# Group-0 chunks of the state-space mixer computed during a reordered convolution, three-block tails split by tokens, and weights loaded ahead of the norms, in a two-layer hybrid block

## The chip, the cores and the metric

The kernel runs on one core of one Trainium2 chip. The metric is the device time of one execution in microseconds. TensorE (PE; its weight loads are PEld), VectorE (DVE), ScalarE (ACT), GpSimd (POOL) and SyncE (SP, which here only issues DMAs) work side by side, each through its own instruction queue in order.

## The reference, cut to what matters

Two layers over 512 latent tokens (`x`) and 256 context tokens (`ctx`) of width 1024. In the last layer only the latent tokens are carried on.

```python
h  = rms_norm(x, w) * (1 + sc_m) + sh_m            # adaLN; the same for the context
ua, ub, ug = split(h @ w_in)                       # neighbourhood attention | SSD | GQA
ya = neighbourhood_attention(ua)
# SSD: z, xbc, dt = split(ub); xbc = silu(depthwise_conv5(xbc)); xs, B, C = split(xbc)
#   per chunk of 128 tokens, both directions, 8 heads in 2 groups:
#   y_diag = ((C B^T) * decay) @ (xs * dt);  y_off = C @ h_enter;  y += d_skip * xs
#   then y * silu(z), RMSNorm
yg = gqa_attention(ug)
x = x + g_m * (concat(ya, yb, yg) @ w_out)
x = x + g_f * swiglu(rms_norm(x) * (1 + sc_f) + sh_f)
```

## The kernel before

Everything is float32. A matrix product is made from three: each operand is split into a rounded high part and the rest, and high*high, high*low and low*high are summed (`proj_ws`, L349; weights stationary, 512 + 256 token columns moving in the first layer, 512 in the last; `proj_as`, L364, has the activations stationary). `load_w` (L341) fetches a weight block by a DMA of SP into a raw buffer (tag `wr`, two of them), ACT writes the high part (L345), DVE the low part (L346), into `wh`/`wl` (three pairs) or `vh`/`vl` (two pairs). A raw buffer is free again when DVE has made the low part. Program order is the order in which raw buffers are asked for. The framework orders the instructions of each engine by a list schedule in program order and by its own clock; `tc.issue_after(i)` puts the instructions of a block behind `i` on `i`'s engine.

A layer runs so. `make_h` (L323) makes the normalised input of 8 blocks of 128 channels. The input projection follows: queries and keys of the neighbourhood attention, `p_kv` (L709), `p_q` (L718), then the eight blocks of the convolution, `p_xbc(b)` (L758), in the order 0 to 7: blocks 0 to 3 are xs (0 and 1 are head group 0), 4 and 5 are B of group 0 and 1, 6 and 7 are C. Between them stand the gate blocks `p_z` (L808), transposes `p_xtr`, `decays` (L821, after block 4), the heads' rotary work, and in the first layer the modulation products `mod_steps` (L213), moved on by `step_md`.

Then comes a loop over attention units (48 in the first layer, 32 in the last): scores into PSUM, maximum (DVE), exponential (ACT), normalisation (POOL, L437), transposes (PE, L447), values (PE, L459). `events` hangs the SSD work between the units by a list of due times (`UCFG`, L25): `diag(c, g)` (L908) computes y_diag of one chunk and one head group in five steps (two DMAs of decay rows into `wh`/`wl`; ACT L920; DVE L924; ACT L926, PE L929, DVE L931 and L932, POOL L935; DVE L939, L940; PE L945, L946 and DVE L948); `steps` (L960) carries the states. There are 12 such pieces in the first layer and 8 in the last.

The output projection adds to the residual in 16 half blocks (`load_wo`, L1228). `tail_blocks` (L1188) handles the last two of the eight column blocks of a sum over all channels by token parts (`tparts`, L525: 512 and 256 tokens in the first layer, 256 and 256 in the last): both blocks for part 0, then block 0 of part 1, the token sums of part 0 (`sums`, L1201, two matmul groups and two DVE operations), block 1 of part 1, then the reciprocal root (a power on POOL, L286, and three small DVE operations, L291, L292 and L294) spread over 128 partitions (`spread`, L311: PE L315, ACT L320). It stands at each layer's second norm (before the feed-forward net), at the end of the feed-forward net and so before the next layer's first norm, and at the very end. In the first layer's feed-forward net DVE also computes the modulation rows (`mod_dots`, L234): 56 steps, each with a 512 KB load into a raw buffer (L240). What is left of them is drained right before the last tail (L1327).

## Time and profile before

| | us |
|---|---|
| runs (3): median, lowest, highest | 1792.51, 1790.63, 1794.35 |
| the profiled execution | 1792.03 |
| its span (first to last instruction) | 1790.3 |
| busy: PE, PEld, DVE | 1735.2, 1472.0, 1025.0 |
| busy: ACT, POOL | 623.6, 265.6 |

Times in rows are microseconds from the first instruction of the span, unless marked ns. PEclk, the granted clock of TensorE, is 1.0 at 2.4 GHz and 0.5 at 1.2 GHz. An idle stretch of an engine is put down to the instruction whose end released it. `S<-HY,wh` reads: output tile `S`, inputs `HY` and `wh`; `L357` is a line of the kernel. SPq is SP's queue of DMA issues.

### The profile page before, as it was taken

The page shows a single profiled execution, that of the slowest core. Times are in us where ns is not written, and L with a number is a line of the kernel's source. Part 1 is how long each engine was busy: PE and PEld are TensorE (multiplying, and loading weights), DVE is VectorE, ACT ScalarE, POOL GpSimd, SP SyncE. Part 2 cuts the span into 40 slices and gives each one's busy share as a digit, 9 for nine tenths or more (in the row PEclk, how much of TensorE's full clock was granted, in tenths as well). Part 3 has the DMA queues.
Part 4 walks back from the last instruction along what each step waited for, and adds up shares of the span by engine and source line. Part 5 has one row for each costly group of instructions (what it writes and reads, how often), then busy time and mean ns, then how long its engine had stood idle before and what let it go on. Part 6 is the DMA issues. An engine that isn't in the chain of part 4 may idle for free.

```text
span 1790.3 us, 26514 instructions
## 1 busy us (share of the span) xinstructions
PE 1735.2 (97%) x10290; PEld 1472.0 (82%) x10290; DVE 1025.0 (57%) x2117; ACT 623.6 (35%) x1202; POOL 265.6 (15%) x289
## 2 busy tenths in 40 slices
PE   7999998999999999999999989999999999999998
PEld 3898886778878888888888878998777888888887
DVE  3645557985575455535554575586895743333335
ACT  4422425665352211221122234334655532232222
POOL 0103116652010000000000011222652100000000
PEclk9999998999989999999999999999999999999999
DMA  9744455522223443333343455233722233333332
GB/s 361 250 130 138 167 159 143 138 89 69 74 86 117 123 121 107 118 105 111 125 122 114 122 162 188 74 108 112 198 63 71 83 107 102 98 93 96 99 106 79
DMA packets 93742, 220.61 MB, mean 123 GB/s; under 512 B 18352, under 2 KB 26160, under 8 KB 93616
## 3 DMA queue, kind: packets, MB, share of 16 engines
q1 hardware_dynamic: 77520, 203.60, 37.3%
q10 hardware_dynamic: 16096, 15.31, 2.6%
q8 instruction: 81, 1.33, 0.3%
q14 instruction: 45, 0.37, 0.1%
HBM read 197.44 MB, written 21.43 MB: 122 GB/s over the span
## 4 chain that ended last, share of the span: by engine, by line
PE 87%; DVE 6%; DMA 3%; ACT 2%; issue 1%; POOL 1%; SPq 0%; ACTq 0%; DVEq 0%; POOLq 0%
PE S L357 66%; PE sm L371 3%; PE PT L371 3%; PE sm L459 2%; PE PT L447 2%; PE PT L357 1%; DMA wr<-in_mod_wT_dram 1%; PE S L411 1%; DVE wh L924 1%; PE S L188 1%; PE S L414 1%; PE PT L188 1%; PE PT L990 1%; PE sm L945 1%; PE sm L946 1%
## 5 line engine op out<-in xcount | busy, mean ns | idle before, releaser
L345 ACT ACTIVATE wh<-wr 128x1024 fp32r<-128x1024 f32 (+2 forms) x204 | 198.0, 972 | 742.6 <-PE S L357 567.0
L346 DVE TENSOR_TENSOR wl<-wr,wh 128x1024 fp32r<-128x1024 f32 (+2 forms) x204 | 227.9, 1118 | 186.4 <-ACT wh L345 184.1
L357 PE MATMUL S<-HY,wh 128*128 128x512 f32 (+1 forms) x716 | 215.9, 359 | 3.9 <-ACT HY L338 3.9
L357 PE MATMUL S<-HY,wl 128*128 128x512 f32 (+1 forms) x716 | 212.5, 354 | 0.3 <-DVE wl L346 0.3
L357 PE MATMUL S<-HZ,wh 128*128 128x512 f32 (+1 forms) x716 | 212.1, 354 | 0.6 <-DVE HZ L339 0.6
L357 PE MATMUL S<-HS,wh 128*128 128x512 f32 (+1 forms) x716 | 211.3, 353 | 0.0
L357 PE MATMUL S<-HS,wl 128*128 128x512 f32 (+1 forms) x716 | 209.3, 350 | 0.0
L286 POOL TENSOR_TENSOR tiny<-tiny,mhalf 128x2 f32<-128x2 f32 (+2 forms) x17 | 27.0, 1590 | 1069.6 <-DVE tiny L1208 1020.6
L245 DVE CUSTOM_DVE_ANT_0 PT<-wr,XFB 128x512 f32<-128x512 f32 x112 | 75.6, 715 | 182.8 <-DMA wr<-in_mod_wT_dram 182.8
L357 PEld LDWEIGHTS S<-HY,wh 128*128 128x128 f32 x716 | 118.7, 191 | 24.0 <-ACT HY L338 4.2
L357 PEld LDWEIGHTS S<-HZ,wh 128*128 128x128 f32 x716 | 118.7, 190 | 22.8 <-DVE HZ L339 2.1
L357 PEld LDWEIGHTS S<-HY,wl 128*128 128x128 f32 x716 | 117.8, 190 | 19.7 <-DVE wl L346 0.6
L357 PEld LDWEIGHTS S<-HS,wh 128*128 128x128 f32 x716 | 116.9, 188 | 18.1
L357 PEld LDWEIGHTS S<-HS,wl 128*128 128x128 f32 x716 | 116.2, 188 | 18.9
L357 PE MATMUL S<-PHA,wh 128*128 128x512 f32 (+1 forms) x358 | 105.6, 352 | 0.0
L357 PE MATMUL S<-PHB,wh 128*128 128x512 f32 (+1 forms) x358 | 104.7, 350 | 0.0
L357 PE MATMUL S<-GX,wh 128*128 128x512 f32 (+1 forms) x400 | 97.7, 350 | 0.4 <-DVE KA L1162 0.4
L437 POOL TENSOR_SCALAR pr<-pr,tiny 128x640 f32<-128x640 f32 (+2 forms) x80 | 72.7, 911 | 98.5 <-DVE tiny L435 89.5
L1309 DVE TENSOR_TENSOR MB<-S,MA 128x768 f32<-128x768 f32 (+1 forms) x42 | 34.6, 824 | 72.0 <-PE S L357 72.0
L357 PEld LDWEIGHTS S<-GX,wh 128*128 128x128 f32 x400 | 65.9, 189 | 11.2 <-DVE KA L1162 0.8
L447 PE MATMUL PT<-c,pr 128*128 128x128 f32 x384 | 65.4, 285 | 9.5 <-POOL pr L437 4.5
L431 ACT ACTIVATE pr<-S,tiny 128x640 f32<-128x640 f32 (+2 forms) x80 | 61.5, 770 | 32.6 <-DVE tiny L424 21.2
(436 smaller groups left out, 3670.1 us busy)
## 6 DMA issues: line engine op xcount, KB each, us to landing
wr<-in_mod_wT_dram SPq DMA_DIRECT2D x56, 512.0 KB, 3.8
wr<-in_w_gate_dram SPq DMA_DIRECT2D x44, 512.0 KB, 3.6
wr<-in_w_up_dram SPq DMA_DIRECT2D x44, 512.0 KB, 3.6
wr<-in_w_blk_dram SPq DMA_DIRECT2D x28, 512.0 KB, 3.8
wr<-in_w_down_dram SPq DMA_DIRECT2D x32, 448.0 KB, 3.4
wr<-in_w_out_dram SPq DMA_DIRECT2D x32, 256.0 KB, 2.8
wr<-in_w_down_dram SPq DMA_DIRECT2D x16, 512.0 KB, 3.5
QN<-in_mod_w_dram SPq DMA_DIRECT2D x24, 256.0 KB, 5.3
```

Source lines behind the costliest of these rows:

```text
L188: PE.matmul(pm[32 * j : 32 * j + 32, 0:512], lhsT=cs[:, k, :], rhs=w[k], start=(k < 4), stop=(k >= 4), tile_position=(0, 32 * j),)
L245: V.tensor_tensor_reduce(out=ptile() if v == 0 else wv, in0=wv, in1=rows[2 * v + hf], scale=1.0, scalar=0.0, op0=ALU.mult, op1=ALU.add, ac ...
L286: POW.tensor_tensor(out=y, in0=v, in1=mhalf[:, 0:n], op=ALU.pow)
L345: S.activation(hi, raw, AF.Copy)
L346: V.tensor_tensor(lo, raw, hi.bitcast(F32), ALU.subtract)
L357: ins = PE.matmul(pt[:, c0:c1], lhsT=w, rhs=xx[:, c0:c1], start=(k == (0 if len(order) == 1 else order[0]) and i == 0), stop=(k == (nk - 1 ...
L371: PE.matmul(pt[:, 0:n], lhsT=s, rhs=w[:, o : o + n], start=(k == 0 and i == 0), stop=(k == KB - 1 and i == 2),)
L431: exps.append(S.activation(p_, st[:, o0:768], AF.Exp, bias=m[:, 2:3], accum_out=m[:, 3:4]).ins)
L437: G.tensor_scalar(out=p_, in0=p_, scalar1=m[:, 4:5], scalar2=1.0, op0=ALU.mult, op1=ALU.mult).ins
L447: PE.transpose(pt[:, k * P : (k + 1) * P], pr[j, qi][:, kk * P : (kk + 1) * P], ident)
L459: PE.matmul(pv[64 * j : 64 * j + 64, 0:P], lhsT=V2(kts[k], j), rhs=ph[j, qi][:, k, :], start=(k == 0), stop=(k == nkt - 1), tile_position= ...
L1309: V.tensor_tensor(gg[:, c0:c1], pu[:, c0:c1], sg[:, c0:c1], ALU.mult)
```

## The change

There are four parts.

1. **Early chunks.** The convolution runs in the order 4, 6, 0, 1, 5, 7, 2, 3, so that B, C and xs of head group 0 are there after four blocks. `decays` stands after the fourth. Beside the other four blocks `early` runs `diag(c, 0)` for five chunks of the first layer (4, 5, 0, 3, 1) and for all four of the last. Their decay rows go to the buffers `KA` and `KB`, the result with the skip term through a small tile to DRAM (`ysp`), and `load_y` fetches it at the first event of the attention loop. In the loop 7 pieces are left of 12, and 4 of 8, over the same due times. The last layer's gate blocks move from the start of the attention into the convolution.
2. **Modulation products** of the first layer load into `XFB`, `YO`, `HD` and `QN` (not `KA`, `KB`), are copied through `MA`, and run earlier, two steps in each of `p_kv` and `p_q`.
3. **Three-block tails.** `tail_blocks` takes three column blocks: all three for part 0, block 0 of part 1, the sums of part 0, block 1 of part 1, the spread, and block 2 of part 1 behind the spread. The two sums are added in PSUM. `make_h` takes the spread row straight from PSUM for the first two blocks.
4. **Early weights.** The first gate and up block are loaded into `vh`/`vl` ahead of the second norm's tail, and the next layer's first two blocks (`wnext`) ahead of the tail of the feed-forward net.

```diff
@@ -212,9 +212,11 @@
     def mod_steps(l, c):
-        w = mod_loads(l, c, XT)
+        w = mod_loads(l, c, ["XFB", "XFB", "YO", "HD"] + ["QN"] * 4)
...
-        ms = mod_products(w, ps_t(), sb_, lambda o, i_: S.activation(o, i_, AF.Copy))
+        m = ma([P, 512])
+        halves = iter((m[:, 0:256], m[:, 256:512]))
+        ms = mod_products(w, ps_t(), lambda: next(halves), lambda o, i_: S.activation(o, i_, AF.Copy))
@@ -312,13 +314,16 @@
-            PE.matmul(
+            ins = PE.matmul(
...
-        return pbs
+        spread_end.append(ins.ins)
+        return pbs, pb[:, 0:n]
...
+    spread_end = []
@@ -331,9 +336,9 @@
-                G.tensor_tensor(out=t1, in0=t1, in1=pbs, op=ALU.mult)
+                G.tensor_tensor(out=t1, in0=t1, in1=pbs[0], op=ALU.mult)
...
-                V.scalar_tensor_tensor(t1, xT[d][:, c0:c1], s_, pbs, ALU.mult, ALU.mult)
+                V.scalar_tensor_tensor(t1, xT[d][:, c0:c1], s_, pbs[int(d < 2)], ALU.mult, ALU.mult)
@@ -514,6 +519,7 @@
+    wnext = None
@@ -556,7 +562,7 @@
-        ws = [wblk(i) for i in range(2)]
+        ws = wnext or [wblk(i) for i in range(2)]
@@ -713,7 +719,7 @@
-            step_md(1)
+                step_md(t % 3 // 2)
@@ -722,7 +728,7 @@
-            step_md(1)
+                step_md(t % 3 // 2)
@@ -806,7 +812,7 @@
         def p_z(g):
-            wz = [load_w(a["w_z"][l, g, i].rearrange("p k c -> p (k c)"), 1024, "w" if last and g else "v") for i in range(2)]
+            wz = [load_w(a["w_z"][l, g, i].rearrange("p k c -> p (k c)"), 1024, "v") for i in range(2)]
@@ -865,32 +871,6 @@
-        p_kv()
-        p_q()
-        zs = [p_z(0), p_z(1)]
-        next(zs[0])
-        vr = tiny(36)
-        V.tensor_scalar(out=vr, in0=ssr, scalar1=1.0 / 64, scalar2=EPS, op0=ALU.mult, op1=ALU.add)
-        yr = rough(vr, 36)
-        for b in range(8):
-            p_xbc(b)
-            step_md(1)
-            if not last:
-                for _ in range((1, 2, 2, 1, 1, 1, 1, 0)[b]):
-                    next(zs[b // 4])
-                if b == 3:
-                    next(zs[1])
-            if b == 4:
-                dtv, EX, ncum, crow, tdt = decays()
-            if b:
-                p_xtr(b - 1)
-            if b < 3:
-                with tc.issue_after(conv_end[b]):
-                    if b == 0:
-                        r = refine(vr, yr, 36)
-                    head_out(b, qnw[l] if b else knw[l], r, ntok if b else NT)
-            if 2 <= b < 5:
-                head_tr(b - 2, ntok if b > 2 else NT)
@@ -905,16 +885,21 @@
         def xsl(g, c):
...
-        def diag(c, g):
+        def diag(c, g, early=False):
...
-            E, Wb = T(sb, "wh", 3, [P, 4, P]), T(sb, "wl", 3, [P, 4, P])
+            if early:
+                E, Wb = (slot(t, F32, (P, 4, P)) for t in ("KA", "KB"))
+            else:
+                E, Wb = T(sb, "wh", 3, [P, 4, P]), T(sb, "wl", 3, [P, 4, P])
...
-            with tc.issue_after(exps[-1]):
+            with ExitStack() as q:
+                if not early:
+                    q.enter_context(tc.issue_after(exps[-1]))
@@ -938,21 +923,78 @@
+            if early:
+                ydst = T(sb, "zt", 2, [P, 256])
+                skip(c, g, ydst)
+            else:
+                ydst = ysl(g, c)
...
-            ydst = ysl(g, c)
...
-        def skip(c):
-            for g in range(2):
-                G.tensor_tensor(
-                    out=ysl(g, c).rearrange("p (h q) -> p h q", q=64), in0=xsl(g, c),
-                    in1=hb(dsk[l][:, 4 * g : 4 * g + 4], 64), op=ALU.mult,
-                )
+            if early:
+                nc.sync.dma_start(ysp[:, c, :], ydst)
...
+        def skip(c, g, dst):
+            G.tensor_tensor(
+                out=dst.rearrange("p (h q) -> p h q", q=64), in0=xsl(g, c),
+                in1=hb(dsk[l][:, 4 * g : 4 * g + 4], 64), op=ALU.mult,
+            )
...
+        dch = ([4, 5] if not last else []) + [0, 3, 1, 2]
+        ech = dch[0 : 5 if not last else 4]
+        ysp = dr.tile([P, 6, 256], F32, name=nm("ysp"), tag=nm("ysp"))
...
+        p_kv()
+        p_q()
+        zs = [p_z(0), p_z(1)]
+        next(zs[0])
+        vr = tiny(36)
+        V.tensor_scalar(out=vr, in0=ssr, scalar1=1.0 / 64, scalar2=EPS, op0=ALU.mult, op1=ALU.add)
+        yr = rough(vr, 36)
+        egs = [diag(c, 0, True) for c in ech]
+        et = 0
...
+        def early(n):
...
+            nonlocal et
+            for _ in range(n):
+                if et == 0:
+                    next(egs[0])
+                et += 1
+                with tc.issue_after(conv_end[-1]):
+                    for k in range(len(egs)):
+                        if 0 < et - 4 * k < 6:
+                            next(egs[k], None)
+                    if et % 4 == 2 and et // 4 + 1 < len(egs):
+                        next(egs[et // 4 + 1])
...
+        order = (4, 6, 0, 1, 5, 7, 2, 3)
+        for i, b in enumerate(order):
+            p_xbc(b)
+            step_md(1)
+            if i == 3:
+                dtv, EX, ncum, crow, tdt = decays()
+            if i >= 4:
+                early((2, 2, 2, 2)[i - 4] if last else (2, 3, 3, 3)[i - 4])
+            for _ in range(((1, 1, 1, 1, 1, 1, 0, 0) if last else (1, 2, 2, 1, 1, 1, 1, 0))[i]):
+                next(zs[i // 4])
+            if i == 3:
+                next(zs[1])
+            if i:
+                p_xtr(order[i - 1])
+            if 4 <= i < 7:
+                early(3 if last else (4, 3, 3)[i - 4])
+            if i < 3:
+                with tc.issue_after(conv_end[i]):
+                    if i == 0:
+                        r = refine(vr, yr, 36)
+                    head_out(i, qnw[l] if i else knw[l], r, ntok if i else NT)
+            if 2 <= i < 5:
+                head_tr(i - 2, ntok if i > 2 else NT)
@@ -1024,6 +1066,10 @@
+        def load_y():
+            for c in ech:
+                nc.sync.dma_start(ysl(0, c), ysp[:, c, :])
@@ -1090,8 +1136,7 @@
-        dch = ([4, 5] if not last else []) + [0, 3, 1, 2]
-        dgs = [diag(c, g) for c in dch for g in range(2)]
+        dgs = [diag(c, g) for c in dch for g in range(2) if g or c not in ech]
@@ -1112,6 +1157,7 @@
+        ev.append((1, -1, load_y))
@@ -1124,21 +1170,19 @@
-        if last:
-            next(zs[1])
-        else:
-            scores(0)
+        scores(0)
...
-            if last and n == 5:
-                scores(0)
-            if n == (6 if last else 1):
+            if n == 1:
+                p_xtr(order[-1])
...
-        skip(dch[0])
+        skip(dch[0], 1, ysl(1, dch[0]))
...
-                skip(c)
+                for g in range(2):
+                    if g or c not in ech:
+                        skip(c, g, ysl(g, c))
@@ -1175,23 +1219,14 @@
-        def token_sums(src, n):
-            pq = ps_sm()
-            for tb in range(n):
-                ins = PE.matmul(
-                    pq[:, tb : tb + 1], lhsT=src[:, tb * P : (tb + 1) * P], rhs=ones[:, 0:1], start=True, stop=True
-                )
-            return pq[:, 0:n], ins.ins
...
         def tail_blocks(load, nk, xh, xl, which, order, then):
-            d0, d1 = KB - 2, KB - 1
-            ws = [load(d) for d in (d0, d1)]
-            pts = [ps_s() for _ in ws]
+            d0 = KB - 3
+            ws = [load(d) for d in range(d0, KB)]
+            pts = [ps_s(), ps_s(), Split()]
...
-            ins = None
@@ -1201,27 +1236,31 @@
             def sums(part, sq):
...
-                qa, _ = token_sums(acc[:, c0:c1], n)
-                qs, ins = token_sums(sq, n)
-                va, v = tiny(n), tiny(n)
-                V.tensor_scalar(out=va, in0=qa, scalar1=1.0 / D, scalar2=EPS, op0=ALU.mult, op1=ALU.add)
-                V.scalar_tensor_tensor(v, qs, 1.0 / D, va, ALU.mult, ALU.add)
-                return rsqrt(v, n), ins
+                pq = ps_sm()
+                for tb in range(n):
+                    for i, src in enumerate((acc[:, c0:c1], sq)):
+                        ins = PE.matmul(
+                            pq[:, tb : tb + 1], lhsT=src[:, tb * P : (tb + 1) * P], rhs=ones[:, 0:1],
+                            start=(i == 0), stop=(i == 1),
+                        )
+                return rsqrt_small(pq[:, 0:n], n, 1.0 / D), ins.ins
             def row(part, r_):
...
-            block(0, tparts[0])
-            _, sq = block(1, tparts[0])
-            for p0, p1 in zip(tparts, tparts[1:]):
-                block(0, p1)
-                r_, ins = sums(p0, sq)
-                with tc.issue_after(ins):
-                    ins, sq = block(1, p1)
-                with tc.issue_after(ins):
-                    row(p0, r_)
-            r_, _ = sums(tparts[-1], sq)
-            row(tparts[-1], r_)
+            p0, p1 = tparts
+            for i in range(3):
+                _, sq = block(i, p0)
+            block(0, p1)
+            r_, ins = sums(p0, sq)
+            with tc.issue_after(ins):
+                ins, _ = block(1, p1)
+            with tc.issue_after(ins):
+                row(p0, r_)
+            with tc.issue_after(ins if fin and last else spread_end[-1]):
+                _, sq = block(2, p1)
+            r_, _ = sums(p1, sq)
+            row(p1, r_)
@@ -1237,7 +1276,7 @@
-        for d in range(KB - 2):
+        for d in range(KB - 3):
@@ -1250,12 +1289,14 @@
+        def load_gu(name, j):
+            return load_w(a[name][l, j].rearrange("p k c -> p (k c)"), 1024, "w" if j else "v")
...
+        wgu = [load_gu(n, 0) for n in ("w_gate", "w_up")]
...
-        def load_gu(name, j):
-            return load_w(a[name][l, j].rearrange("p k c -> p (k c)"), 1024)
@@ -1287,7 +1328,7 @@
-                    ws = [load_gu(n, 0) for n in ("w_gate", "w_up")]
+                    ws = wgu
@@ -1318,7 +1359,7 @@
             def load_dn(d):
...
-            for d in range(KB - 2 if fin else KB):
+            for d in range(KB - 3 if fin else KB):
@@ -1328,6 +1369,8 @@
+                if not last:
+                    wnext = [load_w(a["w_blk"][l + 1, i].rearrange("p k c -> p (k c)"), 1024, "v") for i in range(2)]
```

## Rows read from the trace of the kernel before

**Rows 1.** Engines' busy time, from the profile's page.
```profile
PE 1735.2 (97%) x10290; PEld 1472.0 (82%) x10290; DVE 1025.0 (57%) x2117; ACT 623.6 (35%) x1202; POOL 265.6 (15%) x289
```
**Rows 2.** Stretches: start:end, length, busy (instructions) of PE PEld DVE ACT POOL; PEclk, DMA.
```profile
300.00:420.00 120.00, 112.50 (x883) 90.99 (x882) 104.74 (x285) 76.09 (x215) 70.98 (x90) 1.00 0.43 124
1246.00:1380.00 134.00, 125.36 (x932) 99.41 (x931) 108.74 (x275) 79.18 (x204) 71.27 (x84) 1.00 0.42 118
```
**Rows 3.** Stretches at half clock, columns as above.
```profile
273.79:284.03 10.24, 7.01 (x29) 5.12 (x28) 8.57 (x19) 4.29 (x10) 6.68 (x7) 0.50 0.12 38
495.66:505.90 10.24, 8.41 (x26) 6.61 (x25) 8.81 (x13) 6.46 (x11) 5.58 (x4) 0.50 0.14 48
1072.51:1079.34 6.83, 6.27 (x15) 4.40 (x16) 6.83 (x11) 4.90 (x8) 4.14 (x3) 0.50 0.05 21
1413.84:1420.67 6.83, 5.88 (x27) 5.60 (x27) 6.50 (x17) 4.83 (x11) 2.75 (x4) 0.50 0.27 80
```
**Rows 4.** PE's waits at the first layer's second norm: total us, times, longest.
```profile
PE sm L315 <- DVE tiny L294: 2.7, 1, 2.7
PE S L357 <- ACT HY L338: 1.5, 1, 1.5
```
**Rows 5.** PE's waits from 1042 to 1090, the first layer's last tail.
```profile
PE S L357 <- ACT wh L345: 1.0, 1, 1.0
PE S L357 <- DVE QN L1162: 0.9, 1, 0.9
PE S L357 <- DVE wl L346: 0.7, 1, 0.7
```
**Rows 6.** PE's waits at the last layer's second norm, 1398 to 1432.
```profile
PE sm L315 <- DVE tiny L294: 1.5, 1, 1.5
PE S L357 <- ACT HY L338: 1.0, 1, 1.0
```
**Rows 7.** SP's issues before that tail, two of PE's matmuls: start, us, what [idle before].
```profile
1021.11 0.33 SPq L343 DMA_DIRECT2D wr<-in_w_down_dram  x1
1023.16 7.26 SPq L240 DMA_DIRECT2D wr<-in_mod_wT_dram  x2
1032.14 4.92 SPq L240 DMA_DIRECT2D wr<-in_mod_wT_dram  x2
...
1044.60 0.33 SPq L343 DMA_DIRECT2D wr<-in_w_down_dram  x1
...
1049.02 0.73 PE L357 MATMUL S<-GV,wh 128*128 128x512 f32 x2 [1.03 <-ACT wh L345]
...
1072.35 0.68 PE L357 MATMUL S<-HY,wh 128*128 128x512 f32 x1 [1.49 <-ACT HY L338]
```
**Rows 8.** DMA issues: instructions, KB each, median us to landing.
```profile
wr<-in_w_blk_dram SPq DMA_DIRECT2D x28, 512.0 KB, 3.8
```
**Rows 9.** Costliest groups: shapes, count | busy us, mean ns | idle before.
```profile
L345 ACT ACTIVATE wh<-wr 128x1024 fp32r<-128x1024 f32 (+2 forms) x204 | 198.0, 972 | 742.6 <-PE S L357 567.0
L346 DVE TENSOR_TENSOR wl<-wr,wh 128x1024 fp32r<-128x1024 f32 (+2 forms) x204 | 227.9, 1118 | 186.4 <-ACT wh L345 184.1
```
**Rows 10.** Two stretches of the feed-forward nets, columns as in Rows 2.
```profile
690.00:720.00 30.00, 30.00 (x172) 26.02 (x171) 15.71 (x37) 4.35 (x5) 0.00 (x0) 1.00 0.40 116
1590.00:1620.00 30.00, 30.00 (x134) 24.84 (x133) 9.87 (x11) 7.90 (x10) 0.00 (x0) 1.00 0.34 99
```
**Rows 11.** DVE by line in the first layer's attention, 258 to 420: mean ns.
```profile
L924 DVE SCALAR_TENSOR_TENSOR wh<-wh,dtr,wl 128x128 f32<-128x128 f32 x48 | 22.6, 505 | 0.5 <-ACT wl L920 0.2
L939 DVE TENSOR_TENSOR wl<-wh,SB 128x512 f32<-128x512 f32 x12 | 9.5, 793 | 0.2
```
**Rows 12.** Line L924 in the whole trace: ns min/median/max.
```profile
L924 DVE SCALAR_TENSOR_TENSOR wh<-wh,dtr,wl x80: 328/356/1611, 272.8 to 1336.2; 128x128 f32<-128x128 f32 x80
```
**Rows 13.** The two convolutions, columns as in Rows 2.
```profile
142.00:266.00 124.00, 122.78 (x831) 107.64 (x824) 69.65 (x118) 39.09 (x73) 26.13 (x21) 0.99 0.51 165
1152.00:1232.00 80.00, 80.00 (x498) 71.52 (x497) 63.98 (x97) 30.54 (x53) 22.52 (x16) 1.00 0.32 102
```

## The prediction, made before the changed kernel was run

> **What bounds the kernel now.** First the engines' busy time: PE is busy 97% of the span, the next, DVE, 57% [rows 1]. So the change can win three things only: time in which PE stands idle, time in which it runs at the lower clock, and its own work. It takes no matmul product away; so I looked for the first two, in the busy times by stretch. In the plain feed-forward stretches PE is busy all the time at full clock [rows 10], and nothing is to be had. The two attention loops lose 7.5 us in the first layer (112.50 busy of 120.00) and 8.6 in the last (125.36 of 134.00), with DVE busy 87% and 81% there [rows 2]. Half clock stands in four places that the change touches [rows 3]: at the start of the first attention (10.24 us, PE busy 7.01), at the first layer's second norm (10.24, 8.41), at the norm between the layers (6.83, 6.27) and at the last layer's second norm (6.83, 5.88). At half clock at most half of the busy time is lost: 3.5, 4.2, 3.1 and 2.9 us. The waits of PE then say what ends its idle time at the norms: the reciprocal root (L294) before the spread, and the first block of normalised input (L338) after it [rows 4, 6, 7]. Between the layers there is another kind: PE waits for the weights of the tail itself, 1.0 us for the high part, 0.7 for the low, and 0.9 for an evacuation, 2.6 in all [rows 5].
>
> **The change part by part.** The sum is made against the profiled execution: span 1790.3, time 1792.03, so 1.7 us outside the span; this time lies 0.5 under the median of the runs, 1792.51.
>
> *Rates.* In the first layer 172 matmuls take 30.00 us, a mean of 0.174 over pairs of 512 and 256 columns; in the last 134 of 512 columns take 30.00, 0.224 each [rows 10]. So a pair takes 0.349, and one of 256 columns 0.349 - 0.224 = 0.125.
>
> *Three-block tails, first layer's second norm.* Block 2 of part 1 (12 matmuls of 256 columns, 1.5 us) now stands between the spread and the first product of the feed-forward net. That is as long as the wait for the first input, 1.5 [rows 4], so I put it at nothing. The wait of 2.7 for the reciprocal root has the same cover as before, block 1 of part 1, and DVE can still be taken by weight splits, since three tail blocks now fill all three `wh` pairs and the next block's split starts when the first of them is done; I take 0.3 off. Of the 4.2 lost to the clock I take 2.7: PE was idle and then busy with tiny products before the clock fell, and the new order keeps the first idle stretch. Sum -4.5; bounds -1.5 (the covered wait alone) and -8.4 (all of 2.7 + 1.5 + 4.2). The spread row read from PSUM only starts DVE sooner, inside the covered wait. What is late next is DVE's making of the inputs.
>
> *The norm between the layers.* The same: the wait of 1.49 [rows 7] goes (block 2 is 21 x 0.125 = 2.6 us long here), and as it bridges more than before I take all of the 3.1 of the clock: -4.6, bounds -1.5 and that. But here the **early weights cost**. A raw buffer is asked for in program order, and SP's issues in the trace keep that order: block 5 of the down projection, five modulation loads (two and two in the rows, the fifth left out behind them), then block 6 [rows 7]. With three blocks in the tail, block 5 is itself behind the drain: where it stood there are now five modulation loads and the two early weight blocks. In the trace the six issues from 1021.11 to 1044.60 follow each other by 3.9 us. At that pace block 5 is issued seven places later, at 1048.5; but one of those six steps held its buffer long waiting for a `wh` pair, and modulation loads don't, so the lower end is the time that five of them took after it, 21.4 us, to 1042.5 [rows 7]. I take 1043.5, near that end. It lands 3.6 us later (the block loads' median is 3.8 [rows 8]), and ACT's split takes 1.0 [rows 9]: 1048.1. PE needs it one block before 1049.02 - 1.03 = 1048.0 [rows 7], and a block takes 21 x 0.349 = 7.3: at 1040.7. So a **new wait** of 7.4 us (6.4 to 12.3), in place of the old 2.6, and I add 1.6 for the clock after it (0 to 3.4, half of a stretch of 6.83 [rows 3]): +6.4, bounds -2.6 (if the loads are ahead after all) and +13.1. Both together +1.8.
>
> *The last layer's second norm.* Waits of 1.5 and 1.0 [rows 6], clock 2.9: the second goes, and 1.6 of the clock: -2.6, bounds -1.0 and -5.4. The two early loads here stand in front of the last three output blocks. Each holds a raw buffer for 3.8 + 1.0 + 1.1 = 5.9 us [rows 8, 9], while a block of PE's lasts only 12 x 0.224 = 2.7: blocks 5 to 7 come up to 5.9 later than now. No row shows how far ahead they are; I take +3 (0 to 5.9), the middle. In the first layer a block is 12 x 0.349 = 4.2 long with three pairs ahead, 12.6 in all, so the same 5.9 stay covered: nothing. Sum +0.4.
>
> *The end, and parts of 256.* The last layer's third tail block runs as 256-column halves: 33 matmuls more are halved (12 and 21), at 2 x 0.125 - 0.224 = 0.03 each, +0.9. The last token sums, root and output still come after the last product: nothing.
>
> *The attention loops.* Five of twelve diagonal pieces leave the first loop, four of eight the last. On DVE one costs there 4 x 0.505 (L924) and 2 x 0.79 (L939 and its like) [rows 11], and I estimate another 0.8 for its three small steps: 4.4, so 22 and 18 us of DVE. What PE has of them it has to do elsewhere, which is worth nothing by itself. Only idle time can be won. First layer: 7.5 in the loop and 3.5 at its start by the clock. I take half of each, -5.5 (bounds -11 and +5: the keys of the second head load into `KA` and `KB`, which the last early piece still holds, and this piece follows the last convolution on DVE; such a load lands in some 4 us, by [rows 8], with 1 us for the issue). Last layer: a third of 8.6, -2.9 (bounds -8.6 and +5), since its gate blocks no longer fill PE while the first units start up.
>
> *The convolutions.* DVE is busy 69.65 of 124.00 and 63.98 of 80.00 [rows 13], PE all the time. The early pieces fall in the second halves: by halves some 35 + 22 of 62 us and PE's share of the pieces on top in the first layer, and 32 + 18 of 40 and more in the last. That is at or above nine tenths of DVE, and what is queued behind a diagonal step is the next convolution, whose PSUM tile PE needs two blocks later. I take +2 and +2 (each 0 to +5). ACT waits in order too: an exponential (L926) that waits for L924 holds up the next weight split.
>
> The Trainium skill, SBUF, section "Who interferes with whom", says that DVE and GpSimd share a pair of ports under an exclusive lock, so that a DVE operation with two SBUF inputs and a GpSimd one that reads SBUF wait for each other whole. The trace fits: L924 takes 328 ns at best and up to 1611 [rows 12], with a mean of 505 in the attention [rows 11], where POOL is busy 59%; in the convolution it is busy 21% [rows 2, 13]. By that rule the moved pieces shrink by 4 x 0.15 = 0.6 us each on DVE, and the sum would be about 1 us lower, if DVE is what holds PE there.
>
> *Covered edits.* The modulation products run on other buffers and earlier; PE does as much, and the same buffers are free then; the gate weights in `vh`/`vl`, the sums added in PSUM (one DVE step less off the path) and the five small loads of `load_y` stand beside PE work of many us. If their cover were gone, each is a us at most.
>
> **Sum.** -4.5 + 1.8 + 0.4 + 0.9 - 5.5 - 2.9 + 4 = -5.8. The profiled execution would be 1786.2, and the runs' median 1786.7; I predict 1786.
>
> **The rivals.** (a) *All covers hold*: the weights are there, no new wait. Then -4.5, -4.6 - 2.6, -2.6 and +0.9 at the tails, -8 and -4 in the attentions, +1 in the convolutions: -24, about 1768 (1762 to 1778). For it speaks that tails and attention attack the very waits of PE; against it the order of the issues. (b) *Moving the pieces brings nothing*: PE's idle time in the loops is the latency of a unit (scores, maximum, exponential, POOL, transposes), and 87% of DVE is no bound. Then both attention terms are 0: +2.6, so 1795: no change. (c) *The raw buffers decide, and it is slower*: block 5 is issued at 1048.5 instead of 1043.5, and the last layer's blocks late by the full 5.9. Then the place between the layers gives 12.3 - 2.6 + 3.4 - 1.5 = +11.6, the last layer's norm 5.9 - 1.0 = +4.9, all else as forecast (-8.0): +8.5, 1801. The point from which it decides: block 5's issue later than about 1046, or, in the trace after, a wait of PE for `wh` of over 10 us in one place.
>
> **How the numbers follow.** Forecast (1778 to 1788.9): 0.42. (a): 0.22. (b): 0.20. (c): 0.16. The range takes the forecast, (b), more than half of (a) and half of (c): 1767 to 1800, with about 0.08 left out on either side. Faster by over 0.2%, under 1788.9, about what a measurement of this kernel can tell from no change: 0.42 + 0.22 = 0.64. Within it, up to 1796.1: 0.20. Slower: 0.16.
>
> **What would show it.** Right: no wait of PE for L338 at the three norms; a new wait of PE for `wh` of 6 to 8 us at the first block of the tail between the layers, behind seven loads that SP issues before it; more PE busy in the loops at less DVE; DVE over 85% in the convolutions' second halves. Wrong: half clock as long as before at all norms; the block loads of that tail issued ahead of the drain; a wait at the start of the attentions for keys.

## The result, and the profile after

The changed kernel takes 1856.0 us (1855.0 to 1858.0) where the kernel before takes 1791.6: a ratio of 1.036, interval 1.034 to 1.038. It is 64 us slower; the forecast of 1786 and its range up to 1800 are both missed. The profiled execution has a span of 1856.2 at a mean granted clock of 0.974, against 1790.3 at 0.986.

The engines' busy time after, to be read against [rows 1]:

```profile
PE 1759.4 (95%) x10323; PEld 1489.7 (80%) x10323; DVE 1017.1 (55%) x2115; ACT 626.6 (34%) x1206; POOL 254.6 (14%) x289
```

PE has 33 matmuls more, DVE is no busier; PE's busy time is 24 us longer, since more of it runs at half clock, and PE's idle time is 42 us longer. To find the place, the span is cut at six events that both kernels have: the first convolution block's first step on ACT, the last value product of an attention, and the first spread product at a norm. Each row of the table is read in this way from its kernel's own trace (us), the times are medians:

| kernel | time | A: first conv. block to last values, layer 1 | B: to its norm 2 | C: to the norm between | D: to last values, last layer | E: to its norm 2 | F: to the end |
|---|---|---|---|---|---|---|---|
| before | 1791.6 | 272.7 | 68.4 | 573.6 | 297.5 | 46.2 | 378.1 |
| after | 1856.0 | 297.6 | 66.8 | 583.2 | 323.5 | 50.0 | 379.7 |
| e1 no early pieces | 1817.7 | 269.8 | 66.8 | 579.9 | 313.3 | 51.2 | 380.2 |
| e2 two per layer | 1825.1 | 277.3 | 66.8 | 569.2 | 318.7 | 51.4 | 380.2 |
| e3 no early block weights | 1847.6 | 292.5 | 66.8 | 575.1 | 321.9 | 50.3 | 379.3 |
| e4 tails alone | 1791.2 | 270.1 | 66.8 | 576.6 | 300.2 | 44.9 | 379.3 |
| e5 e1 with z back | 1811.0 | 266.3 | 66.8 | 580.3 | 309.4 | 49.8 | 380.6 |
| e6 buffers exchanged | 1838.1 | 289.5 | 66.8 | 573.2 | 320.4 | 50.3 | 379.6 |
| e7 e4, steps spread | 1785.8 | 273.8 | 66.7 | 569.4 | 300.4 | 44.9 | 379.2 |
| e8 e4, early gate weights | 1797.8 | 270.1 | 66.8 | 575.0 | 300.2 | 51.3 | 380.4 |
| e9 e6, `crow` off SP | 1840.3 | 287.3 | 66.8 | 579.9 | 318.0 | 50.1 | 381.6 |
| e10 after, z loads late | 1835.4 | 286.0 | 66.8 | 570.4 | 321.0 | 49.8 | 380.5 |
| e11 all undone, pieces kept | 1824.0 | 289.2 | 66.8 | 568.7 | 319.1 | 44.9 | 379.4 |
| e12 e11 without pieces | 1790.3 | 267.5 | 66.8 | 567.4 | 308.1 | 45.0 | 379.4 |
| e13 e11, steps sooner | 1810.5 | 285.6 | 66.8 | 570.2 | 306.3 | 44.9 | 378.9 |
| e14 e11 with two per layer | 1811.4 | 282.2 | 66.8 | 567.6 | 316.7 | 44.9 | 379.6 |
| e15 e13, two in layer 1 | 1799.0 | 275.4 | 66.8 | 565.4 | 304.0 | 44.9 | 378.9 |
| e16 e13, last layer only | 1788.9 | 267.8 | 66.8 | 567.9 | 306.3 | 44.9 | 380.3 |

Of the 66 us between the two spans A has 24.9 and D 26.0: the two layers' convolution with attention, where the forecast had -3.5 and -0.9. C has 9.6, E and F 5.4, B -1.6; 1.6 lie ahead of A. Three things limit the reading of the table. Column C also holds up to 10 us of a difference in PE's pace that no edit explains; it is told at the end, and causes under some 10 us are read from the other columns. Column A differs by up to 5.1 us between kernels whose edits lie behind it (after 297.6 and e3 292.5; e4 270.1 and e7 273.8; e1 269.8 and e5 266.3), so a smaller difference in A between two single executions sizes nothing. And the three-block tails move 12 products, some 1.5 us, from B and E behind the spread, into C and F: the 1.6 that B loses is this, and no gain by itself.

Inside A and D, the stretch from the first convolution block to the first scores (lines 3 and 4 below) grew from 103.2 to 130.2 and from 70.7 to 100.4, while the loop from the first scores to the last values (lines 1 and 2) only went from 169.5 to 167.4 and from 134.0 to 126.5. Stretches of after; columns as in Rows 2:

```profile
285.60:453.00 167.40, 150.09 (x1093) 121.64 (x1093) 113.43 (x328) 94.89 (x264) 84.08 (x111) 0.93 0.38 110
1300.00:1426.50 126.50, 118.00 (x864) 92.57 (x863) 91.92 (x238) 71.50 (x179) 70.28 (x85) 0.96 0.40 108
155.40:285.60 130.20, 114.70 (x754) 101.63 (x753) 80.62 (x147) 43.58 (x87) 19.20 (x25) 0.93 0.41 130
1199.60:1300.00 100.40, 88.70 (x564) 79.85 (x564) 68.73 (x120) 35.58 (x68) 19.62 (x20) 0.97 0.37 119
```

DVE is busy 62% and 68% there, and 58% and 64% in the second halves (206 to 262 and 1236 to 1300, below), for which the forecast had nine tenths. Its work grew about as forecast, by 21.3 and 11.3 us against 22 and 18; it is the stretches that got longer.

```profile
206.00:262.00 56.00, 50.41 (x312) 45.37 (x313) 32.52 (x54) 20.35 (x40) 9.68 (x13) 0.94 0.52 163
...
1236.00:1300.00 64.00, 52.30 (x324) 46.57 (x322) 40.71 (x69) 24.04 (x48) 12.72 (x16) 0.95 0.47 150
```

PE, which stood still for 1.2 us of 124 before [rows 13], is idle for 15.5 and 11.7. What it waits for (after; the three windows are 205 to 262, 262 to 346 and 1199 to 1320; total, times, longest):

```profile
PE S L362 <- ACT wh L350: 5.1, 1, 5.1
...
PE S L416 <- ACT pr L436: 8.2, 2, 7.1
PE PT L803 <- ACT GX L809: 4.1, 2, 3.5
PE S L416 <- DMA KA<-nk: 3.1, 1, 3.1
...
PE S L362 <- ACT wh L350: 6.3, 1, 6.3
PE PT L803 <- DVE GT L786: 3.0, 1, 3.0
```

So three kinds are new: convolution weights (`wh`) that come late in the middle of both convolutions, keys (`KA`), and a wait of 7.1 us for an exponential in the middle of the first attention (at 331.71). Half clock stands at each of them: 6.8 us from 216.0 and from 1246.8 at the weights, and these stretches of after (the first around the wait for keys, the second from inside the 7.1 us, the third from inside the wait of 10.1 us at the tail between the layers, below):

```profile
280.90:294.50 13.60, 10.47 (x48) 10.21 (x48) 6.17 (x15) 2.36 (x6) 3.51 (x6) 0.50 0.48 135
335.50:345.70 10.20, 6.92 (x30) 6.93 (x31) 3.73 (x14) 4.49 (x13) 3.83 (x5) 0.50 0.36 103
1072.80:1083.00 10.20, 4.10 (x9) 2.89 (x10) 6.37 (x7) 3.79 (x5) 0.00 (x0) 0.50 0.68 210
```

Summed over the trace, without the stretch at its very end, half clock stands for 95.6 us, twice the 47.8 of before.

The waits at the tail between the layers, 1060 to 1125, which answer to [rows 5] and the L338 of [rows 7], and SP's issues there:

```profile
PE S L362 <- ACT wh L350: 10.1, 1, 10.1
PE S L362 <- DVE HZ L344: 1.8, 1, 1.8
PE S L362 <- ACT HY L343: 1.5, 1, 1.5
```

```profile
1060.51 3.76 SPq L242 DMA_DIRECT2D wr<-in_mod_wT_dram  x2
...
1068.30 3.68 SPq L348 DMA_DIRECT2D wr<-in_w_blk_dram  x2
1074.19 0.33 SPq L348 DMA_DIRECT2D wr<-in_w_down_dram  x1
```

This is the new wait of the forecast: two modulation loads and the next layer's two weight blocks go out before the first weights of the tail, at 1074.19, and PE stands from 1068.84 to 1078.90.

### The profile page after: what moved, and what is told of

Same layout as the page of the kernel before. It is cut to its first block, busy times and chain, and to the rows that moved or that the text cites. A ratio compares the mean times of both kernels' runs of the same rounds, so it can differ in the third digit from the quotient of the medians.

```text
span 1856.2 us, 26615 instructions
## 1 busy us (share of the span) xinstructions
PE 1759.4 (95%) x10323; PEld 1489.7 (80%) x10323; DVE 1017.1 (55%) x2115; ACT 626.6 (34%) x1206; POOL 254.6 (14%) x289
## 4 chain that ended last, share of the span: by engine, by line
PE 84%; DVE 6%; DMA 6%; ACT 2%; issue 1%; POOL 1%; SPq 0%; ACTq 0%; DVEq 0%; POOLq 0%
PE S L362 61%; PE sm L376 3%; PE PT L376 3%; PE sm L464 3%; PE PT L362 2%; PE PT L452 2%; DMA wr<-in_mod_wT_dram 2%; PE S L416 1%; DMA wr<-in_w_blk_dram 1%; PE sm L936 1%; PE sm L935 1%; PE S L419 1%; PE PT L188 1%; DVE wl L351 1%; PE PT L1032 1%
## 5 line engine op out<-in xcount | busy, mean ns | idle before, releaser
L350 ACT ACTIVATE wh<-wr 128x1024 fp32r<-128x1024 f32 (+2 forms) x196 | 189.5, 968 | 757.7 <-PE S L362 557.2
L351 DVE TENSOR_TENSOR wl<-wr,wh 128x1024 fp32r<-128x1024 f32 (+2 forms) x196 | 218.8, 1117 | 215.3 <-ACT wh L350 213.2
L362 PE MATMUL S<-HY,wh 128*128 128x512 f32 (+1 forms) x696 | 206.6, 356 | 11.7 <-ACT wh L350 11.7
L362 PE MATMUL S<-HY,wl 128*128 128x512 f32 (+1 forms) x696 | 207.0, 357 | 0.0
L362 PE MATMUL S<-HZ,wh 128*128 128x512 f32 (+1 forms) x696 | 204.8, 354 | 0.0
L362 PE MATMUL S<-HS,wh 128*128 128x512 f32 (+1 forms) x696 | 202.9, 351 | 0.0
L362 PEld LDWEIGHTS S<-HY,wh 128*128 128x128 f32 x696 | 115.1, 191 | 32.9 <-ACT wh L350 12.3
L362 PE MATMUL S<-PHA,wh 128*128 128x512 f32 x348 | 101.9, 352 | 0.0
L362 PE MATMUL S<-PHB,wh 128*128 128x512 f32 x348 | 101.4, 351 | 0.0
L442 POOL TENSOR_SCALAR pr<-pr,tiny 128x640 f32<-128x640 f32 (+2 forms) x80 | 67.7, 847 | 65.7 <-DVE tiny L440 43.1
L779 DVE SCALAR_TENSOR_TENSOR MB<-S,c,MB 128x770 f32<-128x770 f32 (+3 forms) x64 | 63.0, 984 | 17.1 <-ACT MB L774 16.0
```

What stands on the lines that cost most here:

```text
L350: S.activation(hi, raw, AF.Copy)
L351: V.tensor_tensor(lo, raw, hi.bitcast(F32), ALU.subtract)
L362: ins = PE.matmul(pt[:, c0:c1], lhsT=w, rhs=xx[:, c0:c1], start=(k == (0 if len(order) == 1 else order[0]) and i == 0), stop=(k == (nk - 1 ...
L442: G.tensor_scalar(out=p_, in0=p_, scalar1=m[:, 4:5], scalar2=1.0, op0=ALU.mult, op1=ALU.mult).ins
L779: V.scalar_tensor_tensor(ac[:, s0:s1], pt[:, s0 + j - 2 : s1 + j - 2], convw[l][:, b, j : j + 1], ac[:, s0:s1], ALU.mult, ALU.add,)
```

## The experiments

Line numbers in the text are those of each kernel itself; nothing is left out of the computation in any of them.

**Which part costs what: the pieces, the z products, the weights.** e1 takes the early pieces away and leaves all else; e2 keeps two per layer.

```diff
-        ech = dch[0 : 5 if not last else 4]
+        ech = []            # e1;   e2: ech = dch[0:2]
```

> The changed kernel without early pieces: the convolution's new order, the new place of the z products, the tails and the early weights stay, and all diagonal pieces are back in the attention loops. Theory (the early pieces rotate through the two KA and two KB buffers, and the keys of the attention wait for the last of them): first scores of the first layer back at about 260 (285.6 with the pieces, 257.0 in the kernel before), the last layer's 8 convolution blocks back to some 72 us from the first to the last (93.6 with the pieces); 1856 - 26 - 20 = about 1810. Rival (the reordered convolution or the moved z products cost the time): the convolutions stay as long as they are and the time stays over 1840.

Measured 1817.7: the pieces cost 38.3 us, and A is back at 269.8. D isn't: 313.3 against 297.5 before, with no piece in it. The last layer also shows what the pieces bring where they leave. In e1 the stretch up to the first scores takes 82.2 and the loop 135.8 (below); in after they take 100.4 and 126.5. So the loop does get 9.3 shorter without four pieces, 3.9 of it PE's idle time (12.4 to 8.5), but the stretch ahead of it gets 18.2 longer.

```profile
1250.80:1386.60 135.80, 123.43 (x918) 98.79 (x917) 109.14 (x275) 78.21 (x202) 78.09 (x95) 0.95 0.38 108
```

> The changed kernel with two early pieces in each layer in place of five and four; each has a KA and a KB buffer of its own, so no piece waits for another's buffer. Theory (rotation): the second piece has let go of its buffers before the keys are due, first scores at 262 or before, and nearly all of the gain of the kernel without early pieces is there, 1810 to 1818. Rival (each piece costs DVE and PE time of the convolution, in proportion): two of five and two of four pieces leave 0.45 of the loss, 1828 to 1835.

Measured 1825.1, between the two expectations: 7.4 of the 38.3 stay with two pieces. The profile has 7.5 more in A and 5.4 more in D, and 10.7 less in C, at another pace of PE. So by A and D, which lose 38.0 when all pieces go, two in each layer keep 12.9.

e5 puts the last layer's z products back to its attention's start, on top of e1:

```diff
-            for _ in range(((1, 1, 1, 1, 1, 1, 0, 0) if last else (1, 2, 2, 1, 1, 1, 1, 0))[i]):
-                next(zs[i // 4])
+            if not last:
+                for _ in range((1, 2, 2, 1, 1, 1, 1, 0)[i]):
+                    next(zs[i // 4])
...
-        scores(0)
+        if last:
+            next(zs[1])
+        else:
+            scores(0)
...
+            if last and n == 5:
+                scores(0)
```

> The changed kernel without early pieces, and the last layer's z products where the kernel before has them: four of them (12.2 us of PE at its attention's start) between the first scores and the second unit's. Theory (the products moved into the convolution were the cover of the attention's start, and the loop doesn't get shorter without them: 134.0 before, 135.8 without early pieces and without them): 1817.7 - 11 to - 14 = 1804 to 1807. Rival (PE does them anyway, at either place): within 3 us of 1817.7.

Measured 1811.0: 6.7 us, half of what was expected. In the profiles D has 3.9 of it, and A, where nothing was edited, 3.5. The loop grew from 135.8 to 143.8 when the products came back into it, the convolution fell by 13.0 (first block to first scores, 82.2 to 69.2). So 12 us of products do fill idle time of the loop, but only in part.

e3 takes the next layer's early weights out of the changed kernel; e4 is the kernel before with the three-block tails by parts of the tokens and nothing else; e8 adds the early gate and up weights to e4, and e7 gives out the modulation steps sooner in e4:

```diff
-                if not last:
-                    wnext = [load_w(a["w_blk"][l + 1, i].rearrange("p k c -> p (k c)"), 1024, "v") for i in range(2)]
...
-                step_md(j % 2 if j > 1 else 0)
+                step_md(int(j > 1 and (j % 2 == 1 or j % 4 == 0)))
```

> The changed kernel with the first two weight blocks of the last layer loaded behind the tail of the first layer and not ahead of it. Theory (the early weight blocks stand on SP's queue and in the raw buffers ahead of the tail's own weights): the wait of 10.1 us of PE for wh at 1068.84 falls to under 4, and the time to 1846 to 1850. Rival (the drain of the modulation loads alone makes the tail's weights late, since three blocks lie behind it): the wait stays over 7 and the time falls by under 3.

Measured 1847.6: -8.4, and the wait for `wh` is 3.7 us (10.1 in after), both as the theory said.

> The kernel before with the three-block tails by parts of the tokens and the spread row read from PSUM alone: no early weights, no early pieces, the old convolution order. By the forecast's terms -4.5 at the first layer's second norm, -4.6 between the layers less what the tail weights behind the drain cost (+2 to +6), -2.6 at the last layer's second norm, +0.9 for the halved products: 1792 - 5 to 1792 - 9. Rival (what the changed kernel's trace shows: half-clock stretches and new waits for the low part stand at the norms in place of the old ones): 1791 to 1798.

Measured 1791.2 against 1791.0 (0.9989 to 1.0009): no change, as the rival said. At the first layer's second norm the wait of 1.5 us for the first input is gone, but PE now waits 2.7 for the low part of the inputs, and between the layers for the tail's weights (e4, 484 to 512 and 1025 to 1120):

```profile
PE S L360 <- DVE HZ L342: 2.7, 2, 1.8
PE sm L315 <- DVE tiny L294: 2.4, 1, 2.4
...
PE S L360 <- ACT wh L348: 3.9, 1, 3.9
```

> The kernel with three-block tails alone (1791.2), and the modulation steps of the feed-forward loop given out one earlier at five places, so that no drain of five to six modulation loads stands ahead of the tail's weights between the layers. Theory (the drain makes the tail's weights late): the wait of 3.9 us of PE for wh at 1036.9 and the half-clock stretch of 6.8 behind it go: 1784 to 1788. Rival (raw buffers or DVE then hold up the feed-forward loop, at five other places): 1790 to 1794.

Measured 1785.8, a ratio of 0.9973 (0.9962 to 0.9984), as the theory said. The wait for `wh` is gone, and this is the fastest kernel here. The drain of modulation loads, which the kernel before has too, was worth 5.4 us ahead of a three-block tail. What the earlier steps would bring without that tail wasn't run.

> The kernel with three-block tails alone, and the early gate and up weights of the feed-forward net in both layers. By the forecast they make the last layer's output blocks late by some 3 us and cost nothing in the first: 1793 to 1796. Rival (their cover holds in both layers): 1790 to 1792.

Measured 1797.8, above both expectations: the early gate weights cost 6.6 us, nearly all of it in E (44.9 to 51.3). The wait for late output weights is 2.6 us, as forecast, but behind it the clock falls, which it doesn't in e4 (first E of e4, then E of e8 and the half clock in it; columns as in Rows 2):

```profile
1366.10:1411.00 44.90, 42.41 (x223) 35.42 (x222) 29.11 (x56) 19.79 (x38) 2.14 (x2) 1.00 0.31 90
```

```profile
1364.20:1415.50 51.30, 45.84 (x223) 38.16 (x222) 31.13 (x57) 20.66 (x39) 1.11 (x2) 0.93 0.34 108
1401.90:1408.70 6.80, 6.36 (x28) 6.13 (x29) 3.69 (x7) 2.47 (x5) 0.00 (x0) 0.50 0.60 161
```

**Why the pieces cost 38 us.** The first theory was their buffers: the changed kernel has two `KA` and two `KB`, five pieces go through them, and the keys come behind the last. e6 gives the pieces `XFB`, `YO` and `HD`, and the modulation loads `KA` and `KB` again; e9 moves `crow`'s rows off SP on top of that; e10 is the changed kernel with the z loads six units later.

```diff
-        w = mod_loads(l, c, ["XFB", "XFB", "YO", "HD"] + ["QN"] * 4)
+        w = mod_loads(l, c, XT)                                          # e6
-                E, Wb = (slot(t, F32, (P, 4, P)) for t in ("KA", "KB"))
+                E, Wb = (slot(t, F32, (P, 4, P)) for t in ("XFB", ("YO", "HD")[ech.index(c) % 2]))
...
-                d_ = nc.sync.dma_start(t.rearrange("p h t -> p (h t)"), ...)
+                d_ = (nc.gpsimd if early else nc.sync).dma_start(...)    # e9; crow's stores on nc.scalar
...
-        ev.append((14, 2, load_z))
+        ev.append((20, 2, load_z))                                       # e10
```

> The changed kernel with the buffers exchanged: the early pieces use XFB, YO and HD, and the modulation loads use KA, KB and QN as in the kernel before. So no key waits for a piece, while the pieces still rotate through two pairs among themselves. Theory (the keys wait for the last pieces' buffers): the keys' first loads come back to before 262, first scores to 262 to 272 (285.6), and the time to 1830 to 1840. Rival (the chain of the pieces, five in two pairs, is itself what ends late, with the scores behind it in PE's order): first scores stay over 278 and the time over 1848.

Measured 1838.1, first scores at 264.0: both as the theory wanted, and still the theory isn't what happened. The first scores come 21.6 us sooner than in after, the first value products only 2.4 sooner (299.4 against 301.8), and the loop is 179.0 long instead of 167.4. A falls by 8.1, D by 3.1, and 10.0 of the 17.9 lie in C, where nothing was edited (PE's pace): that the time came out as expected is luck. The keys were not what the attention waited for: three of the five pieces still have their products behind the first scores, at 274.9, 280.0 and 288.3.

> The changed kernel with the loads of the z products issued at unit 20 of the attention loop in place of unit 14. Theory (in the changed kernel they meet the loads of two heads' keys, which come late and close together, and the store of a value block, 11.1 us from issue to landing, makes ACT and then PE wait 7.1 us at 331.7): the wait goes under 2.5 and with the 10.2 us of half clock behind it the time falls by 6 to 12, to 1844 to 1850. Rival (the store is late because of the keys alone): the wait stays over 5, 1853 to 1858.

Measured 1835.4, below both expectations. The wait of 7.1 us is gone, and the longest in that place is 1.3, as expected. A is 11.6 shorter than in after, 6.5 shorter than in e3, which shares after's first layer and has 8.3 for this wait. (Most of the rest of the 20.7 lies in C, where nothing was changed: PE's pace.) The store of a value block from issue to landing, in after and then in e10 (KB, us), and the step of ACT that waits for it in after:

```profile
ydr<-SB ACTq DMA_DIRECT2D x1, 128.0 KB, 11.1
```

```profile
ydr<-SB ACTq DMA_DIRECT2D x1, 128.0 KB, 5.7
```

```profile
337.67 0.28 ACT L650 ACTIVATE SB<-sm 128x128 f32<-128x128 f32 x1 [6.67 <-DMA ydr<-SB]
337.84 0.79 ACT L436 ACTIVATE pr<-S,tiny 128x640 f32<-128x640 f32 x1
```

In after eight loads of keys, two rows of `crow` and two of the four z loads go out from 318.55 to 326, just ahead of the store; the store holds `SB`, ACT waits for `SB`, the next exponential is behind that on ACT, and PE behind the exponential. That e6, where the keys come at another time, loses the same wait without touching the z loads says the same.

> The kernel with the buffers exchanged (1838.1), and the rows of crow off SP: their stores are issued by ACT, which makes them, the early pieces' loads by POOL. Theory (the convolution's weight loads stand on SP behind these stores and loads, which wait for the decays): the waits of PE for wh at 211.6 (4.0) and 1220.9 (5.9) fall under 1.5, and with the half clock behind them the time falls by 9 to 15, to 1823 to 1829. Rival (the weights are late because their raw buffers or the splits on ACT and DVE are): the waits stay, 1835 to 1840.

Measured 1840.3: no gain in the time, and the theory falls, since the waits for `wh` are still 5.7 and 5.7. (A and D are 4.6 shorter together, C is 6.7 longer, at the slower pace.) With the rows issued by POOL, the weight block goes out on SP at 1221.5; it lands 8.6 us later, behind the four rows' 1 MB and two loads of `GR`. A block away from them takes 3.7 (e9, 1217 to 1222; then one block in e16):

```profile
XFB<-crow POOLq DMA_DIRECT2D x2, 256.0 KB, 4.8
wr<-in_w_blk_dram SPq DMA_DIRECT2D x1, 512.0 KB, 8.6
...
YO<-crow POOLq DMA_DIRECT2D x1, 256.0 KB, 5.8
HD<-crow POOLq DMA_DIRECT2D x1, 256.0 KB, 7.9
```

```profile
wr<-in_w_blk_dram SPq DMA_DIRECT2D x1, 512.0 KB, 3.7
```

So it is the transfers that meet, not the places on SP. The Trainium skill, DMA: Bandwidth & Descriptors, section "Issuing engines are not separate DMA queues", says that transfers started by different engines run on the same sixteen DMA engines and interleave there, so that another issuer saves only the time of issuing; this case's trace agrees (8.6 us with POOL as the issuer of the rows, 8.9 in after with SP, from 1237.74 to 1246.65).

**What is left when all this is undone.** e11 keeps the pieces, with e6's buffers and e9's queues, e5's z products, no early weights, and e7's steps; e12 is the same without pieces (with the modulation buffers of the changed kernel and `crow` on SP).

> The early pieces with every cost undone that was found: exchanged buffers, crow's rows off SP, no early weights, the last layer's z products back at its attention's start, the modulation steps spread. Theory (the pieces cost nothing but for these): within 4 us of the same kernel without pieces, which runs beside it. Rival (PE time moved into a convolution that has no idle time is paid there, while the loop is bound by its units' latency): 6 to 14 us above it.

> The same without early pieces: the kernel with three-block tails and spread modulation steps (1785.8) with the convolutions in the new order. Theory (the order costs the 5 us that are left over when the other costs are taken from the whole): 1788 to 1792. Rival (the order is free): 1784 to 1787.

Measured 1824.0 and 1790.3: the pieces still cost 33.7, so the rival was right, and by more than it said. Without them the kernel stands 4.5 over e7, from which it differs by the convolution's order and the modulation steps in the convolutions: D is 7.7 longer, A 6.3 shorter. In the last layer PE idles for 3.5 us between the first convolution block and the first scores, where e7 has no idle time, and two z products that e7 has ahead of the first scores (48 matmuls) stand behind them. What in the new order does this wasn't tested.

Then e13 with the decays two blocks sooner and all steps before the seventh block, and e14 with two pieces:

```diff
-            if i == 3:
+            if i == 1:
                 dtv, EX, ncum, crow, tdt = decays()
+            if i == 3:
+                next(egs[0])
...
-                early((2, 2, 2, 2)[i - 4] if last else (2, 3, 3, 3)[i - 4])
+                early((2, 4, 3, 0)[i - 4] if last else (2, 5, 4, 0)[i - 4])
...
-            if 4 <= i < 7:
-                early(3 if last else (4, 3, 3)[i - 4])
+            if 4 <= i < 6:
+                early((5, 3)[i - 4] if last else (7, 3)[i - 4])
```

> The kernel with early pieces and every found cost undone (1824.0), with the decays two blocks and the first piece's loads one block sooner, and all steps of the pieces given out before the seventh convolution block. Theory (the pieces come too late: in 1824.0 three of five end behind the first scores): no piece's products behind the first scores of the first layer, the loop under 160 us from first scores to last values (176.7), and the time at 1788 to 1800. Rival (the pieces' work is paid in full in the convolution, and the loop is bound by its units): 1812 to 1826.

> The same kernel as 1824.0 with two early pieces in each layer in place of five and four. Theory (late pieces): the first two come in time, and the time is within 5 us of the kernel without pieces (1790.3). Rival (each piece is paid): two of five and two of four pieces cost 0.45 of 33.7, 1803 to 1808.

Measured 1810.5 and 1811.4. Sooner steps bring 13.5 us: the loads of `crow` no longer meet a weight block (no wait for `wh` over 1 us in either convolution), and D, with four pieces in it, is 306.3, no longer than without any. A is still 285.6, and its loop 183.3 long: in the first layer the sooner steps didn't do what they were for, since three of the five pieces have their products at 266.1, 277.3 and 284.1, behind the first scores at 257.5. The two pieces of e14 have the weights late again (6.9 us at 211) and cost more than e2's. Neither time lies in either of its expectations.

> The kernel with the sooner steps (1810.5), with two pieces in the first layer in place of five, four in the last as there. Theory (the pieces that wait for a buffer pair of an earlier one, each some 25 us from one piece's products to the next in the same pair, come out behind the first scores and hold up the first units): the first layer's stretch from the first convolution block to the last values goes from 285.6 to 268 to 272, the time to 1792 to 1798. Rival (each piece is paid alike): two fifths of 18 stay, 1799 to 1804.

> The same with no early piece in the first layer, and four in the last. Theory (in the last layer pieces that come in time are free): 1788 to 1792, as without pieces (1790.3). Rival (they cost there too, and the last layer's 306.3 was a good profile): 1794 to 1800.

Measured 1799.0 and 1788.9 (0.9966 to 0.9996 of before). e16's time is as the theory said, though only two of its four pieces come in time: their products start at 1206.6, 1217.1, 1226.1 and 1236.0, the first scores at 1219.6. Four such pieces cost nothing there, and bring little: D is 306.3 against 308.1 in e12, with the same loop of 144 us. PE's idle time in the loop falls from 10.6 to 6.8, but other products take the pieces' place (e12, then e16):

```profile
1219.00:1363.20 144.20, 133.63 (x1040) 110.41 (x1039) 111.96 (x282) 79.73 (x207) 78.58 (x95) 0.99 0.40 113
```

```profile
1219.90:1364.00 144.10, 137.30 (x1050) 112.17 (x1049) 103.61 (x259) 75.80 (x193) 73.84 (x91) 0.99 0.40 109
```

e15 lies at the rival's edge: A is 267.8 with no piece, 275.4 with two, 285.6 with five, so 3.8 us a piece for the first two and 3.4 for the other three, whether or not a piece needs a buffer twice. (The 7.6 of the first two is not far above what A varies by; the times, 1788.9, 1799.0 and 1810.5, have the same order.) The stretches show part of how (first line of each: first scores to last values; second: the convolution up to the first scores; e12 without pieces, then e15 with two):

```profile
254.30:420.90 166.60, 154.77 (x1183) 125.07 (x1181) 136.22 (x378) 106.08 (x295) 100.51 (x128) 0.98 0.40 118
153.40:254.30 100.90, 99.46 (x667) 88.36 (x666) 59.46 (x97) 31.59 (x57) 8.27 (x8) 0.98 0.40 127
```

```profile
261.30:431.70 170.40, 154.68 (x1164) 123.49 (x1162) 131.38 (x361) 103.06 (x285) 96.22 (x125) 0.96 0.39 110
155.50:261.30 105.80, 103.61 (x691) 91.98 (x690) 64.89 (x115) 35.76 (x68) 14.11 (x17) 0.97 0.49 150
```

The convolution got 4.9 longer, with 4.2 more of PE's busy time: PE had no idle time there to take the products in. The loop lost 19 matmuls and 4.8 us of DVE's work and did not get shorter (its 3.8 more are within what A varies by); PE's busy time in it is the same 154.7, at a lower clock. So of some 3.6 us a piece 2.1 are its products on PE; what the rest is stays open.

**The sum.** From after: pieces -38.3 (e1), z products -6.7 (e5), early weights and drain -20.7 (e12 against e5), order -4.5 (e7): 1785.8. The steps follow each other from kernel to kernel, so they have to add up; only the 20.7 can be checked: 8.4 (e3), 6.6 (e8) and 5.4 (e7), each measured in another kernel, make 20.4. The tails themselves are worth 0 (e4).

## Why the prediction was wrong, point by point

**First layer's second norm, -4.5.** The wait for the first input went, and the root's wait lost 0.3, both as said. But "What is late next is DVE's making of the inputs" was priced at nothing, and it is 2.7 us of waits for the low part in e4, 3.0 in after. The step that failed is the covered wait: the cover let the high part come in time, and the low part, a DVE step behind it, was late instead. Nor did the 2.7 of the clock come back in after: half clock there is 10.2 us, as before (6.8 in e4).

**The norm between the layers, +1.8.** Place and mechanism of the new wait were right: 10.1 us at the first block of the tail, forecast 7.4 (6.4 to 12.3). The mis-sized term is the issue of block 5. PE needs it 28.1 later than the forecast had it (1068.84 against 1040.7), so 1074.19 answers to 1046.1, where 1043.5, near the lower end, was taken. Eight loads went out ahead of it, not seven. Of the -4.6 nothing came: 1.5 and 1.8 us of waits for inputs stand where 1.5 stood. e3 shows that the early blocks have 8.4 of the loss, e7 that the drain alone has 5.4.

**The last layer's second norm, +0.4.** The late output weights were sized well (2.4 us in after, 2.6 in e8, forecast 3), the clock behind them wasn't: forecast -1.6, but the wait brought 6.8 us of half clock in e8 where e4 has none. Early gate weights alone cost 6.6 against the +3.

**The convolutions, +2 and +2.** This is the step that failed most: up to the first scores the two stretches grew by 27.0 and 29.7 us, 13.0 of the second by the z products (e5). They were priced by DVE, whose work came as forecast. What PE does of the pieces was named and put at nothing: "What PE has of them it has to do elsewhere, which is worth nothing by itself". But [rows 13] show PE without idle time there, and in e15 two pieces add 4.2 us to PE's work and 4.9 to the stretch. Two more things were not counted: the 1 MB of `crow` rows that the first two pieces load just when a weight block is wanted (waits of 5.1 and 6.3 us for `wh`, with half clock); and that the pieces' steps come out late: three of five pieces of the first layer have their products within 11 us of the first scores (285.6) or behind them: at 274.7, 279.3 and 286.4. What this lateness costs by itself no run shows, since e13 didn't cure it. Moved transfers were counted at the tails and not here.

**The attention loops, -5.5 and -2.9.** The loops went from 169.5 to 167.4 and from 134.0 to 126.5, the second without 12 us of z products. In the last layer the forecast gain is there: PE's idle time in the loop falls by 3.9 from e1 to after, and by 3.8 from e12 to e16. In the first it isn't: 12.0 in e1, 17.3 in after, 11.8 in e12, 15.7 in e15. There DVE's 87% was no bound, as rival (b) said, for the reason that idle time in the loop is the chain of each unit (no run tests this reason); but (b) kept the +4 of the convolutions. The bound of +5 for keys named a wait that did come (3.1 us), yet e6 shows that it was covered by what came next.

**The z products.** Their new place was seen ("its gate blocks no longer fill PE while the first units start up") and taken as a smaller gain. It was a loss: 6.7 in the time, 3.9 of it in D.

**The signs.** Right: the wait for `wh` behind the loads ahead of it (10.1 us, where 6 to 8 was written). Not seen: DVE over 85% in the second halves, PE busier in the loops (90% and 93%, before 92% and 94%), and no wait for the first input at all three norms (1.5 and 1.4 us are left at the second and third). Of the signs named as wrong, two came: a wait for keys, and half clock at the norms as long as before or longer (10.2, 17.0 and 6.8 us against 10.2, 6.8 and 6.8). Rival (c)'s sign, a wait of over 10 us for `wh` in one place, was there too, but it decided 8 us of 64. No rival had more than +4 in the convolutions; the pieces and the z products that went there cost 45 us.

## What to carry to other kernels

Idle time in a loop is not a gain until the moved work has a place: before moving it, look at the destination's idle time on the bounding engine, and count every transfer that moves along. Here a piece cost 3.4 to 3.8 us in a convolution where PE was full, and nothing in the last layer's, where PE idled for 3.5 us without the pieces (e12) and their loads no longer met a weight block (e16). A cover that is taken away (products at the start of a loop) is a cost, not a smaller gain. And when a tail is widened so that its weights need to come sooner, look first at what stands ahead of them: giving out five loads sooner was worth 5 us, and no part of the change brought as much.
